# Compressed softmax moved forward, the last branch by tiles, and half of each norm's turning given to transposing transfers

## The chip, the cores and the metric

One NeuronCore of a Trainium2 chip runs the whole program. The metric is the device time of one execution in microseconds. The kernel before took 1357.85 us, the median of 3 runs (1355.42 to 1359.24).

## The reference

Two layers work on 256 tokens of width 1024, in fp32. Cut to what matters here, a layer is:

```python
h = h + 0.5 * swiglu(rms_norm(h, norm_g[i, 0]), ffn1_wi[i], ffn1_wo[i])
n = rms_norm(h, norm_g[i, 1])
... = split_cols(n @ w_in[i], IN_SPLITS)
ya = diff_attention(aq, ak, av, ...)
yb = nsa_attention(bq, bkc, bvc, bks, bvs, bkw, bvw, sigmoid(bgate), ...)
yc = swa_sink_attention(cq, ck, cv, ...)
merged = (sigmoid(ga) * (ya @ w_branch[i, 0]) + sigmoid(gb) * (yb @ w_branch[i, 1])
          + sigmoid(gc) * (yc @ w_branch[i, 2]))
h = h + merged @ w_out[i]
h = h + 0.5 * swiglu(rms_norm(h, norm_g[i, 2]), ffn2_wi[i], ffn2_wo[i])
h = h + sigmoid(rms_norm(h, norm_g[i, 3]) @ w_ple_gate[i]) * (p[i] @ w_ple[i])
```

A last `rms_norm` follows. In `nsa_attention` (branch B) a query attends to three sets of keys: 15 compressed blocks (`o_c`), selected blocks (`o_s`) and a window (`o_w`); their outputs are added, each under its gate. The compressed keys and values come from `gelu(blk @ w1) @ w2`, so they exist only after a product over the keys of all tokens.

## The kernel before, in words

**Tiles.** The 256 tokens are two tiles of 128 (`t` = 0 and 1). An operand of a product is held as a high and a low part (`split`: ScalarE rounds the high part, VectorE subtracts), and a product of two such operands is three matmuls (`mul3`, L234: high x high, high x low, low x high). Weights come in pieces of 128 x 1024 (`raw`, 4 buffers) by SP's queue, and each piece is split into `wh` (ScalarE, L228) and `wl` (VectorE, L223), 6 buffers each; `fetch` runs two pieces ahead.

**Products.** `product` (L305) goes through the contraction in steps. Tile 0 takes block `step`, tile 1 block `step - skew`, so that the beginning and the end of a product belong to one tile. When a tile's last block is done, its `done` function is called with a higher priority; then comes the next step. A norm's operand must have the model dimension on the partitions, so the residual sum `h` has to be turned: `residual` (L372) adds a product's 512 columns to `h`, calls `norm.turn(t, c)` (L343: four TensorE transposes into a bank `nt`, then `turned`, L330: four scalings on ScalarE, four subtractions on VectorE) and squares the columns for the norm's sum. The scale of the norm itself is applied later, to the product's result.

**The FFN** turns its gated values another way: `turn_by_dma` (L436) copies the high and the low 16 bits of each fp32 apart (`cut`, VectorE), SP issues a transposing DMA for each (`flip`), and `collect` puts the halves together again (`whole`, VectorE) when the next group of columns is done.

**The attention beside the products.** While projection and gate products run, attention units are emitted beside them: a `Flow` (L156) steps generators. Each call of `flow.tick()`, once for every three matmuls, moves each lane on by its pace (`PACE_B` for branch B); `flow.join(side)` steps until a side is finished. `attend_b` (L839) works through six units (group g, tile t, key sets), the softmax of one ahead of the weighting of the one before. At the end of a tile's last key set it waits for the compressed keys (`kc`, made by `compressed`, L736, in a second lane at pace 1.0), runs `attend_cmp(t)` (L803: scores `sc`, softmax `pc`, transpose `pct` to `pcT`) if the tile hasn't one, spreads `pcT` over the heads (`own`, L830), weights, and gathers `y_ps` into `yB[t]`. One PSUM bank holds `y_ps`.

**Order.** `attention` (L504) emits the projections, then branch 0 (differential), the compression, branch 2 (window with sinks) and last branch 1 (B). A branch is, for each half of the columns, a gate product `gate` (from the norm) and a product `br` (from `yT`); `mix` multiplies and adds to `merged`. In the last branch both gate products come first, then the join, then both `br` products, each over both tiles with a skew of 4; `mix` there also transposes `merged` (`mt`) and splits it into `mT`, the operand of the output product `wo`, whose `done` feeds the next norm. The program's order is only a priority: a planner in the framework, which estimates durations, lays down the order of instructions of each engine, and each engine then follows that order.

Of the kernel before, what the change touches and what calls it, by code (L numbers as in the profile page):

```python
# [10 lines left out]
F32 = mybir.dt.float32  # L11
F32R = mybir.dt.float32r
U16 = mybir.dt.uint16
# [17 lines left out]
AHEAD = 2  # L31
RAWS = 4
WBUFS = 6
PACE_A, PACE_B, PACE_C = 0.75, 0.75, 0.6

# [118 lines left out]
class Flow:  # L156
# [19 lines left out]
                    lane[1] -= 1.0  # L176
                    self.step(lane)

    def join(self, side):
        while any(s is side for lane in self.lanes.values() for s, _ in lane[0]):  # L180
            for lane in self.lanes.values():
                if lane[0]:
                    self.step(lane)
# [3 lines left out]
def trunk(ctx: ExitStack, tc: tile.TileContext, a: dict, out: bass.AP, index: list):  # L187
# [105 lines left out]
    def last_product(lhs, nk, done, name, w):  # L293
# [8 lines left out]
                done(t, ps, s)  # L302
        return run

    def product(lhs, nk, done, name, w, skew=SKEW):  # L305

        def run():
            ps = [None] * NT
            for step in range(nk + skew):
                for t, k in ((0, step), (1, step - skew)):  # L310
                    if 0 <= k < nk:
                        wh, wl = w(k)
                        if k == 0:
                            ps[t] = product_bank(f"{name}{t}")
                        xh, xl = lhs(t, k)
                        mul3(ps[t][:, :w.width], xh, xl, wh, wl, k == 0, k == nk - 1)
                        if k == nk - 1:
                            with tc.high_priority(offset=150):
                                done(t, ps[t])
                        flow.tick()  # L320
        return run


    class Norm:
# [16 lines left out]
                                               T[:, 0, k + m, :].bitcast(F32), op0=ALU.mult, op1=ALU.subtract)  # L341

        def turn(self, t, c):  # L343
            ps = tp_bank("nt")
            transposes(ps, [h[:, t, 512 * c + 128 * k:512 * c + 128 * k + 128] for k in range(4)])
            self.turned(t, 4 * c, ps)
# [82 lines left out]
            queue.dma_start(out[t * 128:(t + 1) * 128, 512 * k:512 * k + 512], y[k])  # L429


    def halves(x):

        return x.bitcast(U16).rearrange("p (n w) -> p n w", w=2)

    def turn_by_dma(pool, src, m):  # L436


        cut = stage("cut").bitcast(U16).rearrange("p (w n) -> p w n", w=2)
        flip = pool.tile([128, 2, 4, 128], U16, tag="flip", bufs=3, name="flip")  # L440
        for w in range(2):
            nc.vector.tensor_copy(cut[:, w, :128 * m], halves(src)[:, :128 * m, w])
            nc.sync.dma_start(flip[:, w, :m], cut[:, w, :128 * m], transpose=True)

        def collect():
            whole = stage("whole")
            for w in range(2):
                tc.keep_in_program_order(nc.vector.tensor_copy(  # L448
                    halves(whole)[:, :128 * m, w], flip[:, w, :m].rearrange("p a b -> p (a b)")))
            return whole[:, :128 * m].rearrange("p (k q) -> p k q", q=128)  # L450
        return collect

    def ffn(i, n, norm, after, aside=None):
        pool = None
        gT, held, pending = [None] * NT, {}, {}

        def begin():
            nonlocal pool
            pool = phase("ffn")
            for t in range(NT):  # L460
                gT[t] = pool.tile([128, 2, NF, 128], F32R, name=f"gT{t}")

        def collect(t):
            if t in pending:
                first, m, whole = pending.pop(t)
                split(gT[t][:, 0, first:first + m, :], gT[t][:, 1, first:first + m, :], whole())

        def gated(f):
            def done(t, ps):
                collect(t)  # L470
                if f % 2 == 0:
                    held[t] = pool.tile([128, 512], F32, tag="gated", bufs=4, name="gated")
                act = pool.tile([128, 256], F32, tag="act", bufs=3, name="act")
                nc.scalar.activation(act, ps[:, :256], AF.Silu, scale=norm.r(t))  # L474
                nc.vector.tensor_tensor(held[t][:, 256 * (f % 2):256 * (f % 2) + 256], act, ps[:, 256:], op=ALU.mult)  # L475
                if f % 2 or f == FG - 1:
                    first, m = f - f % 2, 2 * (f % 2 + 1)
                    pending[t] = 2 * first, m, turn_by_dma(pool, held[t], m)
            return done

        def gathered(t, k):
            if k == 8:
                collect(t)
            return gT[t][:, 0, k, :], gT[t][:, 1, k, :]

        steps = []

        def beside():
            if not steps:
                steps.append(aside(pool))  # L490
            next(steps[0])

        yield begin
        for f in range(FG):
            yield product(norm.lhs, NK, gated(f), "ff", streamed(i, f"{n}{f}", 512), 2 if aside and f == 0 else SKEW)
            if aside and f in (4, 5, 8):
                yield beside
        for c in range(2):
            if aside and c == 1:
                yield beside  # L500
            yield product(gathered, NF, after(c), "fo", streamed(i, f"{n}o{c}", 512))


    def attention(i, norm, after):  # L504
# [205 lines left out]
        def compress():  # L710
# [14 lines left out]
            for kv in range(2):  # L725
                for k in range(16):
# [3 lines left out]
                    nc.tensor.matmul(o, both, wh, start=k == 0, stop=False)  # L730
                    nc.tensor.matmul(o, both, wl, start=False, stop=k == 15)
                    flow.tick()
            c_sb[0] = pool.tile([128, 512], F32, name="c_sb")
            nc.vector.tensor_copy(c_sb[0][:64], c_ps[:64])

        def compressed():  # L736
# [44 lines left out]
            vc[0] = pool.tile([128, 1, 128], F32R, name="vc")  # L781
            values(vc[0], v_ps[:, :64], None)
            kc[0] = kt

        def weighted(y_ps, v, T, start, stop):

# [11 lines left out]
            v = tmp.rearrange("p (m q) -> p m q", m=2)  # L798
            split(y[:, 0, 2 * g:2 * g + 2, :], y[:, 1, 2 * g:2 * g + 2, :], v)

        yB, pcT = [None] * NT, {}

        def attend_cmp(t):  # L803
            s_ps = tp_bank("sc")
# [34 lines left out]
        def attend_b():  # L839
# [33 lines left out]
            def second(u, p):  # L873
                g, t, ss = u
                if yB[t] is None:
                    yB[t] = y_tile("yB")
                if ss[0] == 0:
                    y_ps[g, t] = y_bank("yb")
                for x in ss:
                    for k in range(t + 1):  # L880
                        T = turned([p[:, j, x, :] if t == 0 else p[:, j, 128 * k:128 * k + 128] for j in range(4)])
                        yield
                        weighted(y_ps[g, t], vB[0][:, x, k, g], T.rearrange("p x j q -> p x (j q)"), x == 0 and k == 0, False)
                        yield
                if ss[-1] == 1:
                    if t not in pcT:
                        while kc[0] is None:
                            yield
                        yield from attend_cmp(t)
                    T = own(t, g)  # L890
                    yield
                    weighted(y_ps[g, t], vc[0][:, 0], T.rearrange("p x j q -> p x (j q)"), False, True)
                    gather(yB[t], y_ps[g, t], g)
                    yield

            yield from pipelined([(g, t, ss) for t, sets in ((0, [(0, 1)]), (1, [(0,), (1,)])) for g in range(2) for ss in sets], first, second)
# [57 lines left out]
        def branch(b, yT, side, last=False):  # L954
# [32 lines left out]
            if last:  # L987
                for c in range(2):
                    yield gated(c, both[c][0])
                yield lambda: flow.join(sides[side])  # L990
                for c in range(2):
                    yield mixed(c, both[c][1])
            else:
                for c in range(2):
                    yield gated(c, both[c][0])
# [236 lines left out]
```

## Time and profile before

| | |
|---|---|
| median of 3 runs | 1357.85 us (1355.42 to 1359.24) |
| profiled execution | 1356.52 us, span 1354.7 us from the first to the last instruction |
| TensorE (PE) busy | 1331.4 us, 98% of the span, 6414 matmuls |
| weight loads of TensorE (PEld) | 1096.5 us, 81% |
| VectorE (DVE) busy | 947.4 us, 70% |
| ScalarE (ACT) busy | 782.2 us, 58% |
| mean granted clock of TensorE | 0.995 |

A matmul's record is longer than its turn, since matmuls are pipelined and their ends are modelled; what one costs in a stream is read from the starts of two neighbours. "Idle before" is the engine's idle time just ahead of an instruction, and the arrow names what ended it.

### The profile page before, as it was taken

The numbers are of one execution on the slowest core, as the hardware profiler recorded it, in microseconds if no ns is written. First come the engines' busy times: TensorE is split into PE (matmuls) and PEld (weight loads), VectorE is DVE, ScalarE is ACT, GpSimd is POOL, SyncE is SP. The second block draws the span as 40 slices with busy tenths as digits, with TensorE's granted clock in tenths as the row PEclk, the third lists the DMA queues.
The fourth block names the chain that finished last, engine by engine and source line by source line (L and its number), as shares of the span: only waits on it lengthen the run. The fifth ranks groups of instructions, "written<-read, shape, count | busy, mean of one in ns | idle before, by whom it ended". The sixth has DMA issues, their size and how long they took to land.

```text
span 1354.7 us, 18246 instructions
## 1 busy us (share of the span) xinstructions
PE 1331.4 (98%) x6414; PEld 1096.5 (81%) x6414; DVE 947.4 (70%) x1795; ACT 782.2 (58%) x1382; POOL 18.5 (1%) x36
## 2 busy tenths in 40 slices
PE   9999999999998999999999999999999989999997
PEld 7778888887886788888888888888788868888886
DVE  7677566768887767665767765577697776767565
ACT  7555455668655655544755544566795645545454
POOL 0000000000000000000000000000000000000000
PEclk9999999999999999999999999999999989999999
DMA  8797665444642577775567765645456425887662
GB/s 306 205 275 224 194 226 169 152 166 155 231 154 64 185 201 220 206 221 180 189 198 216 229 202 193 227 151 177 162 186 205 140 65 184 220 222 210 194 204 84
DMA packets 121993, 257.14 MB, mean 190 GB/s; under 512 B 56944, under 2 KB 62500, under 8 KB 121902
## 3 DMA queue, kind: packets, MB, share of 16 engines
q1 hardware_dynamic: 121150, 254.34, 60.5%
q0 software_dynamic: 320, 1.08, 0.3%
q8 instruction: 50, 0.82, 0.2%
q10 hardware_dynamic: 432, 0.56, 0.1%
q14 instruction: 41, 0.34, 0.1%
HBM read 243.33 MB, written 1.08 MB: 180 GB/s over the span
## 4 chain that ended last, share of the span: by engine, by line
PE 92%; DVE 3%; DMA 2%; ACT 2%; issue 1%; SPq 0%; POOLq 0%; POOL 0%; DVEq 0%; ACTq 0%
PE ff L236 11%; PE ff L237 11%; PE ff L235 11%; PE fo L236 6%; PE fo L235 6%; PE fo L237 6%; PE gate L235 3%; PE gate L237 3%; PE gate L236 3%; PE s L537 3%; PE A L236 2%; PE A L235 2%; PE A L237 2%; PE br L236 1%; PE br L235 1%; PE br L237 1%
## 5 line engine op out<-in xcount | busy, mean ns | idle before, releaser
L223 DVE TENSOR_TENSOR wl<-raw,wh 128x1024 fp32r<-128x1024 f32 (+1 forms) x448 | 539.8, 1213 | 176.5 <-ACT wh L228 169.3
L228 ACT ACTIVATE wh<-raw 128x1024 fp32r<-128x1024 f32 (+1 forms) x448 | 467.6, 1050 | 231.6 <-PE fo L237 84.9
L236 PE MATMUL ff<-wl,nT 128*128 128x512 f32 x704 | 273.6, 390 | 2.0 <-DVE wl L223 1.9
L237 PE MATMUL ff<-wh,nT 128*128 128x512 f32 x704 | 273.4, 390 | 0.0
L235 PE MATMUL ff<-wh,nT 128*128 128x512 f32 x704 | 270.8, 391 | 0.0
L236 PEld LDWEIGHTS ff<-wl,nT 128*128 128x128 f32 x704 | 132.2, 188 | 31.3 <-DVE wl L223 4.0
L235 PEld LDWEIGHTS ff<-wh,nT 128*128 128x128 f32 x704 | 132.4, 188 | 29.3 <-ACT wh L228 0.8
L237 PEld LDWEIGHTS ff<-wh,nT 128*128 128x128 f32 x704 | 132.3, 188 | 27.1
L236 PE MATMUL fo<-wl,gT 128*128 128x512 f32 x352 | 134.2, 392 | 0.0
L237 PE MATMUL fo<-wh,gT 128*128 128x512 f32 x352 | 133.7, 389 | 0.0
L235 PE MATMUL fo<-wh,gT 128*128 128x512 f32 x352 | 132.5, 389 | 0.0
L474 ACT ACTIVATE act<-ff,stats 128x256 f32<-128x256 f32 x88 | 41.4, 472 | 86.0 <-PE ff L237 85.8
L475 DVE TENSOR_TENSOR gated<-act,ff 128x256 f32<-128x256 f32 x88 | 36.6, 417 | 65.0 <-ACT act L474 65.0
L235 PEld LDWEIGHTS fo<-wh,gT 128*128 128x128 f32 x352 | 66.1, 188 | 13.9
L235 PE MATMUL gate<-wh,nT 128*128 128x512 f32 x192 | 77.0, 403 | 0.0
L237 PEld LDWEIGHTS fo<-wh,gT 128*128 128x128 f32 x352 | 66.1, 188 | 13.3
L236 PEld LDWEIGHTS fo<-wl,gT 128*128 128x128 f32 x352 | 66.1, 188 | 13.3
L236 PE MATMUL gate<-wl,nT 128*128 128x512 f32 x192 | 75.9, 395 | 0.0
L237 PE MATMUL gate<-wh,nT 128*128 128x512 f32 x192 | 75.8, 395 | 0.0
L228 ACT ACTIVATE gT<-whole 128x512 fp32r<-128x512 f32 (+1 forms) x48 | 28.4, 591 | 62.8 <-DVE whole L448 62.6
L548 ACT ACTIVATE p<-p,st 128x128 f32<-128x128 f32 (+1 forms) x128 | 56.7, 445 | 11.4 <-DVE st L546 11.0
L448 DVE COPY whole<-flip 128x512 uint16<-128x512 uint16 (+1 forms) x96 | 38.2, 434 | 12.8 <-DMA flip<-cut 12.2
(301 smaller groups left out, 2003.2 us busy)
## 6 DMA issues: line engine op xcount, KB each, us to landing
raw<-in_wst SPq DMA_DIRECT2D x438, 512.0 KB, 4.4
band<-table SPq DMA_DIRECT2D x10, 512.0 KB, 4.9
raw<-in_wbv SPq DMA_DIRECT2D x4, 420.0 KB, 3.2
flip<-cut SPq DMA_TRANSPOSE x96, 4.0
xt<-in_xt SPq DMA_DIRECT2D x4, 256.0 KB, 5.2
raw<-in_wst SPq DMA_DIRECT2D x4, 256.0 KB, 3.5
h<-in_x SPq DMA_DIRECT2D x2, 512.0 KB, 7.9
band<-table POOLq DMA_DIRECT2D x2, 512.0 KB, 6.7
```

The costliest lines, as they stand in the source:

```text
L223: nc.vector.tensor_tensor(o, x, y, op=ALU.subtract)
L228: nc.scalar.activation(hi, src, AF.Copy)
L235: nc.tensor.matmul(ps, xh, wh, start=start, stop=False)
L236: nc.tensor.matmul(ps, xh, wl, start=False, stop=False)
L237: nc.tensor.matmul(ps, xl, wh, start=False, stop=stop)
L448: tc.keep_in_program_order(nc.vector.tensor_copy(halves(whole)[:, :128 * m, w], flip[:, w, :m].rearrange("p a b -> p (a b)")))
L474: nc.scalar.activation(act, ps[:, :256], AF.Silu, scale=norm.r(t))
L475: nc.vector.tensor_tensor(held[t][:, 256 * (f % 2):256 * (f % 2) + 256], act, ps[:, 256:], op=ALU.mult)
L537: nc.tensor.matmul(o, q[r, x, qb[m], t * 128:(t + 1) * 128], kk, start=x + y == 0, stop=x == 1)
L548: nc.scalar.activation(p[j], p[j], AF.Exp, bias=st[:, j:j + 1], scale=-1.0, accum_out=st[:, n + j:n + j + 1])
```

## The change

The diff makes four edits.

- `attend_cmp(t)` of both tiles is stepped at the end of `compressed`, in the second lane; `attend_b` now waits until `pcT[t]` is there. `PACE_B` goes from 0.75 to 0.72, and `c_sb` shares the buffers of `th`.
- The last branch's `br` products go by tiles: `tile(0)` (both halves of the columns) once both groups of `yB[0]` are gathered (`readyB[0] == 2`), then the full join, then `tile(1)`. The weight pieces of both halves are read twice.
- `Norm.turn` with `c == 0` no longer uses TensorE: it calls `turn_by_dma` on `h`'s first 512 columns and puts the collect and `turned` off by 12 steps of `product` (`later`, `on_time`).
- `flip` moves to the pool that lives through the program, with 2 buffers in place of 3.

```diff
-PACE_A, PACE_B, PACE_C = 0.75, 0.75, 0.6
+PACE_A, PACE_B, PACE_C = 0.75, 0.72, 0.6
...
-    def join(self, side):
-        while any(s is side for lane in self.lanes.values() for s, _ in lane[0]):
+    def join(self, side, ready=lambda: False):
+        while not ready() and any(s is side for lane in self.lanes.values() for s, _ in lane[0]):
...
+    deferred = []
+
+    def later(steps, act):
+
+        deferred.append([steps, act])
+
+    def on_time():
+        for d in deferred:
+            d[0] -= 1
+        while deferred and deferred[0][0] <= 0:
+            deferred.pop(0)[1]()
+
...
             for step in range(nk + skew):
+                on_time()
...
+        flip = base.tile([128, 2, 4, 128], U16, tag="flip", bufs=2, name="flip")
...
         def turn(self, t, c):
+            if c == 0:
+                whole = turn_by_dma(h[:, t, :512], 4)
+                later(12, lambda: self.turned(t, 0, whole().rearrange("p k q -> p (k q)")))
+                return
...
-        flip = pool.tile([128, 2, 4, 128], U16, tag="flip", bufs=3, name="flip")
...
-            c_sb[0] = pool.tile([128, 512], F32, name="c_sb")
+            c_sb[0] = pool.tile([128, 512], F32, tag="th", bufs=4, name="c_sb")
...
             kc[0] = kt
+            yield
+            for t in range(NT):
+                yield from attend_cmp(t)
...
-                    if t not in pcT:
-                        while kc[0] is None:
-                            yield
-                        yield from attend_cmp(t)
+                    while t not in pcT:
+                        yield
...
                     gather(yB[t], y_ps[g, t], g)
+                    readyB[t] += 1
...
                 for c in range(2):
                     yield gated(c, both[c][0])
+                ws = [streamed(i, f"br{b}{c}", 512) for c in range(2)]
+
+                def tile(t):
+                    for c in range(2):
+                        ps = product_bank(f"br{t}")
+                        for k in range(4):
+                            wh, wl = ws[c](k)
+                            mul3(ps, yT[t][:, 0, k, :], yT[t][:, 1, k, :], wh, wl, k == 0, k == 3)
+                            flow.tick()
+                        with tc.high_priority(offset=150):
+                            both[c][1](t, ps)
+
+                yield lambda: flow.join(sides[side], lambda: readyB[0] == 2)
+                yield lambda: tile(0)
                 yield lambda: flow.join(sides[side])
-                for c in range(2):
-                    yield mixed(c, both[c][1])
+                yield lambda: tile(1)
```

## Rows read from the trace of the kernel before

**Rows 1.** The page, busy time by engine, and the chain that ended last.
```profile
PE 1331.4 (98%) x6414; PEld 1096.5 (81%) x6414; DVE 947.4 (70%) x1795; ACT 782.2 (58%) x1382; POOL 18.5 (1%) x36
...
PE 92%; DVE 3%; DMA 2%; ACT 2%; issue 1%; SPq 0%; POOLq 0%; POOL 0%; DVEq 0%; ACTq 0%
```

**Rows 2.** Timeline of PE at one turned block: start, duration, what, idle before.
```profile
461.13 0.39 PE L236 MATMUL wo<-wl,mT 128*128 128x512 f32 x1
461.35 0.39 PE L237 MATMUL wo<-wh,mT 128*128 128x512 f32 x1
461.59 0.60 PE L243 MATMUL nt<-ident,h 128*128 128x128 f32 x4
461.94 0.48 PE L235 MATMUL wo<-wh,mT 128*128 128x512 f32 x1
462.25 0.40 PE L236 MATMUL wo<-wl,mT 128*128 128x512 f32 x1
```

**Rows 3.** Stretches: length, busy PE, PEld, DVE, ACT, POOL; clock, DMA share, GB/s.
```profile
350.00:410.00 60.00, 60.00 (x307) 49.35 (x306) 45.64 (x109) 33.99 (x63) 0.00 (x0) 1.00 0.51 171
410.00:450.00 40.00, 33.89 (x166) 26.09 (x165) 32.87 (x66) 22.06 (x44) 0.00 (x0) 1.00 0.29 93
450.00:470.00 20.00, 20.00 (x97) 16.55 (x96) 14.32 (x26) 14.17 (x28) 0.55 (x1) 1.00 0.56 183
1080.00:1120.00 40.00, 34.45 (x156) 27.26 (x155) 31.20 (x64) 20.14 (x41) 0.00 (x0) 0.91 0.31 97
```

**Rows 4.** Timeline of PE, end of the attention of layer 0.
```profile
422.25 0.50 PE L788 MATMUL yb<-pT,vB 128*128 128x512 f32 x1
425.57 0.33 PE L243 MATMUL pct<-ident,pc 128*128 128x128 f32 x1 [2.81 <-DVE pc L822]
...
427.65 0.50 PE L787 MATMUL yb<-pcT,vc 128*128 128x512 f32 x1 [0.45 <-ACT pcT L228]
...
430.71 0.47 PE L787 MATMUL yb<-pT,vB 128*128 128x512 f32 x1 [0.47 <-DVE yt L797]
...
445.31 1.09 PE L243 MATMUL mt<-ident,merged 128*128 128x128 f32 x8 [0.63 <-DVE merged L969]
446.66 0.50 PE L235 MATMUL wo<-wh,mT 128*128 128x512 f32 x1 [0.25 <-ACT mT L231]
```

**Rows 5.** Timeline of PE, the same place in layer 1.
```profile
1090.25 0.50 PE L788 MATMUL yb<-pT,vB 128*128 128x512 f32 x1
1094.10 0.48 PE L243 MATMUL pct<-ident,pc 128*128 128x128 f32 x1 [3.35 <-DVE pc L822]
```

**Rows 6.** Groups by line: count, then busy us, mean ns, idle before.
```profile
L243 PE MATMUL nt<-ident,h 128*128 128x128 f32 x112 | 16.8, 272 | 0.0
```

**Rows 7.** The page's group of `whole`, and the view of tile `flip` (ns min/median/max).
```profile
L448 DVE COPY whole<-flip 128x512 uint16<-128x512 uint16 (+1 forms) x96 | 38.2, 434 | 12.8 <-DMA flip<-cut 12.2
...
L443 SPq DMA_TRANSPOSE flip<-cut x96: 1179/1210/2118, 31.4 to 1261.6; - x96
...
DMA to landing us min/median/max: 2.3/4.0/7.4
```

**Rows 8.** Timeline, from the output product to the next FFN in layer 0.
```profile
456.57 0.69 DVE L377 SCALAR_TENSOR_TENSOR h<-wo,h 128x512 f32<-128x512 f32 x1 [0.40 <-PE wo L237]
...
467.30 0.39 PE L235 MATMUL ff<-wh,nT 128*128 128x512 f32 x1
```

**Rows 9.** Timeline around 65 us.
```profile
64.73 0.39 PE L235 MATMUL ff<-wh,nT 128*128 128x512 f32 x1
65.17 0.45 DVE L448 COPY whole<-flip 128x512 uint16<-128x512 uint16 x1 [0.26 <-DMA flip<-cut]
...
66.79 0.50 PE L236 MATMUL ff<-wl,nT 128*128 128x512 f32 x1 [1.68 <-DVE wl L223]
```

**Rows 10.** Tile `pc` alone, by stretches: length, busy PE, PEld, DVE, ACT.
```profile
410.00:450.00 40.00, 0.33 (x1) 0.14 (x1) 1.69 (x6) 0.29 (x1) 1.00 0.29 93
```

**Rows 11.** Waits of PE: total us, times, longest.
```profile
PE ff L236 <- DVE wl L223: 1.9, 2, 1.7
```

More of the change, by code (lines that the diff above doesn't have):

```diff
@@ L321, in product, with halves, turn_by_dma, collect @@
         return run
+    def halves(x):
+        return x.bitcast(U16).rearrange("p (n w) -> p n w", w=2)
+    def turn_by_dma(src, m):
+        cut = stage("cut").bitcast(U16).rearrange("p (w n) -> p w n", w=2)
+        flip = base.tile([128, 2, 4, 128], U16, tag="flip", bufs=2, name="flip")
+        for w in range(2):
+            nc.vector.tensor_copy(cut[:, w, :128 * m], halves(src)[:, :128 * m, w])
+            nc.sync.dma_start(flip[:, w, :m], cut[:, w, :128 * m], transpose=True)
+        def collect():
+            whole = stage("whole")
+            for w in range(2):
+                tc.keep_in_program_order(nc.vector.tensor_copy(
+                    halves(whole)[:, :128 * m, w], flip[:, w, :m].rearrange("p a b -> p (a b)")))
+            return whole[:, :128 * m].rearrange("p (k q) -> p k q", q=128)
+        return collect
     class Norm:
@@ L429, in finished @@
             queue.dma_start(out[t * 128:(t + 1) * 128, 512 * k:512 * k + 512], y[k])
[L432 to L439, printed above, removed]
-        flip = pool.tile([128, 2, 4, 128], U16, tag="flip", bufs=3, name="flip")
[L441 to L451, printed above, removed]
     def ffn(i, n, norm, after, aside=None):
@@ L477, in done @@
                     first, m = f - f % 2, 2 * (f % 2 + 1)
-                    pending[t] = 2 * first, m, turn_by_dma(pool, held[t], m)
+                    pending[t] = 2 * first, m, turn_by_dma(held[t], m)
             return done
@@ L799, in gather @@
             split(y[:, 0, 2 * g:2 * g + 2, :], y[:, 1, 2 * g:2 * g + 2, :], v)
-        yB, pcT = [None] * NT, {}
+        yB, pcT, readyB = [None] * NT, {}, [0] * NT
         def attend_cmp(t):
```

## The prediction

> **What bounds the kernel now.** I read the page's busy line and its chain first [rows 1]: TensorE is busy 1331.4 of 1354.7 us, and the chain that ended last is 92% PE. In the long products one 512-column matmul starts some 0.23 us after the other, with no wait between [rows 2]. So the time falls only where TensorE gets less to do, or where it stands still. For the second I read the busy time by stretches [rows 3]: TensorE is full in 350:410 and 450:470, but idle for 6.1 us in 410:450 and 5.6 us in 1080:1120, the end of the attention in either layer. The rows inside these stretches [rows 4, 5] name the waits: the transpose of the compressed softmax (`pct`) waits 2.81 us for VectorE's `pc` L822, a `yb` matmul behind it waits 0.45 us for `pcT`, and at the end `mt` waits 0.63 us for `merged` and `wo` 0.25 us for `mT`.
>
> **Part 1, transposes off TensorE.** Seven norms (four of layer 0, three of layer 1; the last one of all is not turned) times two tiles of tokens lose the four `nt` transposes of the first 512 columns. Of the 112 on TensorE [rows 6] half go, 14 groups of four. What a group costs is read from starts [rows 2]: it starts at 461.59, the next product matmul at 461.94, the one behind that at 462.25: 0.66 us in place of one pitch of 0.23, so 0.43 to 0.44 us, and 14 x 0.44 = 6.2 us. TensorE is full there and nothing comes in their place, so this counts in full: -6.2 us.
>
> Added for each group: two `cut` and two `whole` copies on VectorE, and two transposing DMAs on SP. The FFN's gated values go the same way already, with 96 such DMAs [rows 7]: a `whole` copy takes 0.43 us (I take the same for a `cut`), an issue holds SP for 1.21 us, the landing comes 4.0 us after the issue (2.3 to 7.4). VectorE gets 56 copies, 56 x 0.43 = 24 us; it is busy for 947.4 of 1354.7 us [rows 1], and in 450:470, the tightest of the stretches concerned, for 14.3 of 20 us [rows 3], to which 1.7 us come for each of the two turned blocks. SP gets 28 issues of 1.21 us; weight loads queued behind them on SP are late by as much, which the raw buffers already loaded cover; without that cover a pair would cost up to 2.4 us. ScalarE and VectorE still do the four scalings and four subtractions of each half tile, now from SBUF; I cost that difference at nothing.
>
> Is the path in time? The collect is put off by 12 steps. The tightest place lies between the output product `wo` and the next FFN: the sum h starts at 456.57 and takes 0.69 us, the first FFN matmul starts at 467.30 [rows 8]. From 457.3: first cut 0.4, two issues 2.4 (the second cut lies beside the first), landing 2.8 after the second issue ends (4.0 less 1.2), two copies 0.9, scaling and subtraction some 2.3: 466.1, 1.2 us ahead of the need. With the latest landing, 7.4, it is 469.5, 2.2 us late. Behind a late landing the `whole` copies wait in VectorE's order, and the weight splits (`wl`) behind them. In the trace `whole` waits 12.2 us over 96 copies [rows 7], and one such wait reached TensorE: two starts 2.06 us apart at 64.73, where `wl` stood behind a waiting `whole` [rows 9]. The ends of this cost are nothing and 14 x 2.06 = 28.9 us. I take 1 us in all, near the low end, since it lies nearest to the rows of the same operation: 96 copies made one stall of 2 us, so 28 more make a third of one, and the rest is for the three tight boundaries (two from `wo` to an FFN, one from layer 0's gated addition to layer 1's FFN).
>
> The Trainium skill ("VectorE: DVE Perf Modes", section "Rules for kernel authors") speaks against this edit: a 128x128 transpose belongs on TensorE where a PSUM destination will do, and goes by the DMA crossbar otherwise; its section "The three transpose paths" gives 390 against 1309 ns. By its two figures each of the 56 turned blocks would lose 0.9 us, an estimate of 51 us if all of it lay open. The rows above bear that out for the duration of the path (0.66 us against some 9), not for what it costs while other products cover it.
>
> **Part 2, compressed softmax forward.** `attend_cmp(1)` stood in the attention's own lane, inside the second tile's units; now it follows `attend_cmp(0)` at once, in the lane of the compression. The instructions are the same; they move to where TensorE is full whatever VectorE does (45.6 of 60 us busy in 350:410 [rows 3]), which hides the 1.7 us that the `pc` operations take on VectorE [rows 10]; were VectorE full there, they would cost just that. What goes: the wait at `pct`, 425.57 - 422.25 - 0.23 = 3.1 us in layer 0 and 1094.10 - 1090.25 - 0.23 = 3.6 us in layer 1 [rows 4, 5], and the wait for `pcT`, 0.45 us a layer. In layer 1 the granted clock is 0.91 in this stretch, against 1.00 in layer 0 [rows 3]: after the longer standstill TensorE ran at the lower level, 1.2 GHz, for a while. That should go with the wait; I count nothing for it. What is late next is the last unit's softmax; with the `pc` operations gone from among its own it is earlier, and branch matmuls of tile 0 can fill.
>
> **Part 3, last branch by tiles.** Tile 0's 24 branch matmuls need only `yB` of tile 0 and now come before the join; tile 1's 24 follow. `wo` starts with tile 0, whose `mT` is then ready a whole tile earlier, so the waits of `mt` and `wo` go: 0.63 + 0.25 = 0.9 us a layer [rows 4], covered by tile 1's matmuls (24 x 0.23 = 5.5 us). Both weight pieces are held over two tiles: four of the six split buffers, which leaves two for `wo` ahead. Its third piece can be split once tile 1 has used the first, and the second half of tile 1 (2.7 us) covers that; uncovered it would cost about as much.
>
> Parts 2 and 3 together: 3.1 + 0.45 + 0.9 = 4.5 us in layer 0, 3.6 + 0.45 + 0.9 = 5.0 in layer 1, 9.5 in all. Bounds: nothing (another wait steps in), and all idle time of the two stretches, 11.7 us, with a fifth more that the modelled ends hide and the clock's part, about 15. I take 9.5.
>
> PACE_B 0.72 for 0.75, one `flip` buffer less (the two tiles never hold more than two) and `c_sb` in buffers of another name: the pace shifts the attention by 4% of its steps, inside covered work; I cost the three at nothing, with 2 us to either side in the range.
>
> **Sum.** The profiled execution took 1356.52 us (span 1354.7): 1356.5 - 6.2 - 9.5 + 1.0 = 1341.8. It lies 1.3 us under the median of the runs, 1357.85; on that scale 1343.1.
>
> **Rivals.**
> (a) The end of the attention refills: there is one bank for `yb`, so a unit's matmuls wait until the one before is gathered (0.47 us at 430.71 [rows 4]), and the last unit's softmax becomes the late one. For it: VectorE is busy 32.9 of 40 us there [rows 3]. Against: its work there gets less. Only the transposes are gained: 1357.85 - 6.2 + 1.0 = 1352.6.
> (b) The transfers are late at the tight boundaries, so that the longer path lies open there: 2.2 us at each of three, 6.6 us, eat part 1: 1357.85 - 9.5 - 6.2 + 6.6 = 1348.8. Against it: the 1.2 us of margin at the median landing. It is the way in which the rule quoted above from the Trainium skill would come true here.
> (c) The edit doesn't do what it says: the order on each engine comes from a planner, which may leave the compressed softmax late, and (b) eats the rest: about 1357. For it: `pct` ran behind all gate products though its lane is stepped among them.
> (d) Slower: each collect stands ahead of a weight split on VectorE and waits for its landing, so that TensorE stands still in all 14 places as at 64.73 [rows 9]. It decides from (6.2 + 9.5 + 4.1)/14 = 1.4 us a place; at 2.06 us the time is 1357.85 - 15.7 + 28.9 = 1371.1. Against it: the FFN's matmuls waited for `wl` only 1.9 us in all [rows 11], beside 96 such copies.
>
> **How the numbers follow.** Forecast 0.58, (a) 0.17, (b) 0.08, (c) 0.08, (d) 0.09. The forecast's own range is 1337 to 1348: down by 5 (all idle time) and 1 (free collects), up by half of the attention's gain. For 8 in 10, with 2 us more for the pace below, up to (c) above and without (d): 1334 to 1356. A change under 0.3% (4.1 us) can't be told from none here. Faster: the forecast, (b) and most of (a), 0.79; within 0.3%: (c) and the rest of (a), 0.12; slower: (d), 0.09.
>
> **What would show it.** The changed profile should have 56 `nt` transposes, 124 transposing DMAs, `pct` ahead of the last gate matmuls with no wait at it, a granted clock of 1.00 at the end of layer 1's attention, `mt` of tile 0 ahead of tile 1's branch matmuls, and some 6 us less of TensorE's busy time. I am wrong if product matmuls wait several us for a `wl` behind `whole`, or if the two stretches keep over 3 us of idle time each.

## The result, and the profile after

The changed kernel takes 1348.4 us (median of 4 runs, 1345.44 to 1349.38); the kernel before took 1357.55 us beside it (4 runs). The ratio is 0.993, interval 0.9908 to 0.9951. That is faster by 9.15 us, where 14.8 were forecast; the time lies 0.4 us above the forecast's own range of 1337 to 1348 us and inside the wider one, 1334 to 1356. The profiled execution took 1345.44 us, the least of the four, with a span of 1343.7 us: 11.1 us under the profiled execution of before.

The page of the changed kernel, its busy line, its chain, the line of the `whole` copies and that of the transposing transfers; the first two answer to [rows 1], the third and fourth to [rows 7]:

```profile
PE 1321.1 (98%) x6358; PEld 1087.4 (81%) x6358; DVE 965.0 (72%) x1851; ACT 784.5 (58%) x1382; POOL 19.6 (1%) x36
...
PE 88%; DVE 6%; DMA 3%; issue 1%; ACT 1%; SPq 0%; POOLq 0%; POOL 0%; DVEq 0%; ACTq 0%
...
L352 DVE COPY whole<-flip 128x512 uint16<-128x512 uint16 (+1 forms) x124 | 49.6, 438 | 19.0 <-DMA flip<-cut 18.6
...
flip<-cut SPq DMA_TRANSPOSE x124, 4.1
```

56 matmuls are gone from TensorE, 56 operations have come to VectorE, and 124 transfers turn blocks, as predicted. TensorE's busy time fell by 10.3 us, more than the 6 of the transposes: without part 1 (`softmax_tiles` below, 1325.7 us) it is already 5.7 us lower, with as many matmuls as before. VectorE's part of the chain has doubled, 3% to 6%.

Busy time of each engine in stretches of the changed kernel (start:end and length in us, busy time of each engine with its instructions, granted clock, DMA share, GB/s). It answers to [rows 3]; the stretch of layer 1 is taken 5 us wider at the front here, since the work lies earlier:

```profile
350.00:410.00 60.00, 60.00 (x309) 49.71 (x308) 47.99 (x116) 34.99 (x62) 0.00 (x0) 1.00 0.54 176
410.00:450.00 40.00, 35.85 (x180) 28.16 (x180) 31.00 (x63) 21.86 (x47) 0.00 (x0) 1.00 0.32 99
450.00:470.00 20.00, 19.17 (x87) 15.24 (x86) 17.36 (x39) 14.44 (x30) 1.11 (x2) 1.00 0.76 224
1075.00:1120.00 45.00, 40.84 (x202) 32.27 (x201) 33.72 (x65) 24.79 (x46) 0.00 (x0) 1.00 0.36 110
```

The two ends of the attention stand idle for 4.15 and 4.16 us. 450:470, full before, has lost 0.83 us, and VectorE is busy there for 17.36 us in place of 14.3. What TensorE waits for in the changed kernel, longest sums first, cut to what matters here (sum in us, times, longest):

```profile
PE mt L243 <- DVE merged L988: 3.4, 2, 1.7
PE yb L807 <- DVE yt L817: 1.9, 4, 0.8
...
PE ff L236 <- DVE wl L223: 1.5, 2, 1.3
PE nt L243 <- DVE h L415: 1.4, 2, 0.7
PE wo L235 <- ACT mT L231: 1.4, 2, 0.7
PE ff L235 <- ACT nT L370: 1.2, 3, 0.6
PE wo L236 <- DVE wl L223: 1.2, 2, 0.6
```

The wait of `pct` has gone, but `mt` now waits up to 1.7 us [rows 4: 0.63], and three waits are new: `nt` for the sum h, FFN matmuls for `nT`, and `wo` for a weight part `wl`, 0.6 us in each layer. The last is there without part 1 too (1.2 us in two places).

**An account by starts.** Summed over all matmuls, I took the distance from each start to the next, less the pitch of its kind in a stream, that is the distance between two starts where nothing waits (0.227 us for 512 columns, 0.11 to 0.13 for the narrow ones). What is over is time lost to waits, to changes from one kind of matmul to another or to a lower clock. In us:

| | before | softmax and tiles, no turning | changed | changed, no copies |
|---|---|---|---|---|
| sum of the pitches | 1308.4 | 1308.4 | 1302.3 | 1302.3 |
| lost in 350:450 (end of attention, layer 0) | 10.2 | 5.7 | 6.6 | 5.7 |
| lost in 450:500 (`wo` to FFN, layer 0) | 0.2 | 0.1 | 1.5 | 0.0 |
| lost in 650:700 (gated addition to FFN) | 0.2 | 0.1 | 1.1 | 0.0 |
| lost in 1050:1150 (the same two places, layer 1) | 11.1 | 5.4 | 7.7 | 5.3 |

The columns in the middle and at the right are experiments told of below. By their pitches (56 x 0.109) the transposes saved 6.1 us, the forecast's 6.2. The attention saved 4.5 and 5.7 us where it was changed alone; the 11.1 of before hold a stretch of 6.8 us, from 1092.7, in which the granted clock was at its lower level, 1.2 GHz. Then the turning took back 0.9 + 1.4 + 1.0 + 2.3 = 5.6 us in these four stretches.

### The profile page after: what moved, and what is told of

The parts are those of the page before. It is cut to its first block, busy times and chain, and to the rows that moved or that the text cites. A ratio compares the mean times of both kernels' runs of the same rounds, so it can differ in the third digit from the quotient of the medians.

```text
span 1343.7 us, 18223 instructions
## 1 busy us (share of the span) xinstructions
PE 1321.1 (98%) x6358; PEld 1087.4 (81%) x6358; DVE 965.0 (72%) x1851; ACT 784.5 (58%) x1382; POOL 19.6 (1%) x36
## 4 chain that ended last, share of the span: by engine, by line
PE 88%; DVE 6%; DMA 3%; issue 1%; ACT 1%; SPq 0%; POOLq 0%; POOL 0%; DVEq 0%; ACTq 0%
PE ff L237 10%; PE ff L235 10%; PE ff L236 10%; PE fo L237 6%; PE fo L236 6%; PE fo L235 6%; PE gate L235 3%; PE gate L237 3%; PE gate L236 3%; PE s L554 2%; DVE wl L223 2%; PE A L235 2%; PE A L236 2%; PE A L237 2%; PE br L236 1%
## 5 line engine op out<-in xcount | busy, mean ns | idle before, releaser
L228 ACT ACTIVATE wh<-raw 128x1024 fp32r<-128x1024 f32 (+1 forms) x448 | 468.3, 1050 | 229.5 <-PE fo L237 81.9
L237 PE MATMUL ff<-wh,nT 128*128 128x512 f32 x704 | 273.5, 390 | 0.0
L237 PEld LDWEIGHTS ff<-wh,nT 128*128 128x128 f32 x704 | 132.3, 188 | 27.2
L237 PE MATMUL fo<-wh,gT 128*128 128x512 f32 x352 | 134.8, 389 | 0.0
L237 PEld LDWEIGHTS fo<-wh,gT 128*128 128x128 f32 x352 | 66.1, 188 | 13.5
L237 PE MATMUL gate<-wh,nT 128*128 128x512 f32 x192 | 76.1, 396 | 0.0
L352 DVE COPY whole<-flip 128x512 uint16<-128x512 uint16 (+1 forms) x124 | 49.6, 438 | 19.0 <-DMA flip<-cut 18.6
```

Of the source, the lines that this page charges most:

```text
L228: nc.scalar.activation(hi, src, AF.Copy)
L237: nc.tensor.matmul(ps, xl, wh, start=False, stop=stop)
L352: tc.keep_in_program_order(nc.vector.tensor_copy(halves(whole)[:, :128 * m, w], flip[:, w, :m].rearrange("p a b -> p (a b)")))
```

## The experiments

Each ratio is to the kernel before, run beside it on the same chip; its medians there lay between 1357.2 and 1358.2 us.

**1. The change taken apart.** Part 1 alone on the kernel before (in this run and the next three `c_sb` and `flip` have the buffers of the changed kernel, for room):

```diff
+            if c == 0:
+                whole = turn_by_dma(h[:, t, :512], 4)
+                later(12, lambda: self.turned(t, 0, whole().rearrange("p k q -> p (k q)")))
+                return
```

> The kernel before with part 1 alone (the first 512 columns of each norm turned by transposing transfers; c_sb in the buffers of th, for room). By the prediction's terms: -6.2 for the transposes, +1.0 for the collects, 1352.3 us on the scale of 1357.5. By the trace of the changed kernel (the new standstills at the three boundaries, 1.5 + 1.1 + 1.5 us between starts, belong to this part): -6.1 + 4.1, about 1355.5. TensorE's idle time ahead of nt and ff at 460, 670 and 1120 us is there in the second case and not in the first.

Measured: 1355.16 us against 1358.06, ratio 0.9982 (0.9972 to 0.9992). A gain of 2 to 3 us, not the 5.2 of the forecast's terms. At the end of layer 0's attention `mt` waits 2.75 us in it, where it waited 0.63 before [rows 4]; no copy of part 1 stands near, and part 2 alone shows the same wait (below), so this isn't the copies' price.

Part 2 alone, the compressed softmax in the other lane, with `PACE_B` 0.72:

```diff
             kc[0] = kt
+            yield
+            for t in range(NT):
+                yield from attend_cmp(t)
...
-                    if t not in pcT:
-                        while kc[0] is None:
-                            yield
-                        yield from attend_cmp(t)
+                    while t not in pcT:
+                        yield
```

> The kernel before with part 2 alone (compressed softmax in the lane of the compression, PACE_B 0.72; both br products over both tiles as before, turning by TensorE). By the prediction's terms: 3.1 + 3.6 + 0.9 = 7.6 us less, 1349.9. Rival: the part that moves the end of the attention is the order by tiles, and a softmax that comes earlier only lets VectorE's other work be the late one: 1356 or more. Either way no wait of pct at the end of the attention.

Measured: 1347.89 us, 0.992 (0.9908 to 0.9932), 10 us faster.

Part 3 alone, the last branch by tiles (its last lines; `tile` is as in the change):

```diff
...
+                yield lambda: flow.join(sides[side], lambda: readyB[0] == 2)
+                yield lambda: tile(0)
                 yield lambda: flow.join(sides[side])
-                for c in range(2):
-                    yield mixed(c, both[c][1])
+                yield lambda: tile(1)
```

> The kernel before with part 3 alone (last branch by tiles). By the prediction's terms: 0.9 us a layer, 1355.7. Rival, from the changed kernel's trace (mt waits 2.1 us and wo 0.96 us behind tile 1's last branch matmuls, more than before): going by tiles uses up tile 0's wo matmuls as filler ahead of tile 1, so that nothing is left to cover tile 1's chain from br over merged and mt to mT: no gain or slower, 1357.5 to 1360.

Measured: 1351.82 us, 0.995 (0.9936 to 0.9963), 6 us faster; I had given it 1.8.

Parts 2 and 3 without part 1:

```diff
-            if c == 0:
-                whole = turn_by_dma(h[:, t, :512], 4)
-                later(12, lambda: self.turned(t, 0, whole().rearrange("p k q -> p (k q)")))
-                return
```

> The changed kernel without part 1 (turning by TensorE as before). By the prediction's terms 1357.5 - 9.5 = 1348.0. By the trace of the changed kernel, where the ends of the attention lost 3.1 and 3.9 us of standstill: 1350.5. If part 1 is worth what the sum of terms says, this is 5.2 us slower than the changed kernel's 1348.4, 1353.6; if part 1 gives back 4.1 of its 6.1 us, it is 2 us slower.

Measured: 1346.46 us, 0.991 (0.9896 to 0.9923), 12 us faster. Two things follow. Part 1 adds nothing measurable to this. And the gains of parts 2 and 3 don't add up: 10 and 6 us alone, 12 together. TensorE's idle time at the two ends of the attention, in the profiled executions (us):

| | before | part 2 alone | part 3 alone | both |
|---|---|---|---|---|
| 410:455 (layer 0) | 6.1 | 5.4 | 5.7 | 3.2 |
| 1075:1120 (layer 1) | 5.6 | 2.3 | 3.8 | 3.2 |

In layer 1 each edit alone takes away much of the standstill, and the gains overlap. In layer 0 neither takes away much alone: each left what the other would have removed. The longest waits at the end of layer 0's attention, first with part 2 alone, then with part 3 alone (rows of the timeline of TensorE: start, duration, what, idle before):

```profile
444.06 1.95 PE L243 MATMUL mt<-ident,merged 128*128 128x128 f32 x12 [2.75 <-DVE merged L984]
```

```profile
427.75 0.47 PE L243 MATMUL pct<-ident,pc 128*128 128x128 f32 x1 [3.34 <-DVE pc L835]
```

With part 2 alone `pct` no longer waits, but TensorE has nothing beside the last `mt` and waits 2.75 us there: the forecast's "what is late next". VectorE does both `th` additions and a weight split there before the first `merged`; in layer 1 of the same run `merged` comes right behind the first `th`, and `mt` waits 0.60 us. With part 3 alone the wait of `pct` stays in layer 0; in layer 1 it is 0.98 us. Why the planner's order differs between the layers wasn't looked into.

**2. Where the gain of part 1 goes.** The changed kernel once more, unaltered, as the yardstick beside the next three:

> The changed kernel itself, beside the three others of this chip: 1348, and slower than softmax_tiles (the changed kernel without part 1: 0.991 of before), so that part 1 is worth nothing or less on top of parts 2 and 3, though the sum of the prediction has it at -5.2 us.

Measured: 1346.44 us against 1358.15, 0.9919 (0.9905 to 0.9932).

Turning by transfers only in the norms that follow an FFN, where another product covers it; the norms behind `wo` and behind the gated addition turn on TensorE as before:

```diff
-            if c == 0:
+            if c == 0 and self.row % 4 in (1, 3):
```

> The changed kernel with the transposing transfers only in the norms that follow an FFN (4 norms, 8 groups); the norms behind wo and behind the gated addition (3 norms, 6 groups) turn by TensorE as before. If what part 1 gives back is lost at those three boundaries: softmax_tiles' time less 8 x 0.44 = 3.5 us, some 1343, faster than the changed kernel by 4 to 5. If each collect costs something wherever it stands: no faster than softmax_tiles, 1346 or more.

Measured: 1342.86 us, 0.9892 (0.9877 to 0.9907). Half of the edit is worth more than all of it: of 14 turned groups 6 were given up (2.6 us of transposes), and the time still fell by 3.6 us (the slowest of these 4 runs took 1344.12 us, the fastest of the changed kernel beside them 1345.38).

No copies and no transfers (the first 512 columns go on unturned, so part of the computation is left out):

```diff
-                whole = turn_by_dma(h[:, t, :512], 4)
-                later(12, lambda: self.turned(t, 0, whole().rearrange("p k q -> p (k q)")))
+                later(12, lambda: self.turned(t, 0, h[:, t, :512]))
```

> The changed kernel with the 12-step deferral kept, but the scalings read h itself: no cut and whole copies and no transposing transfers in the norms (the first 512 columns are not turned, which is left out here). If VectorE's copies or the landing hold TensorE up at the boundaries: softmax_tiles' time less all of 6.2 us, some 1340.5. If it is the order that comes of collecting 12 steps late: about the changed kernel's time, 1346 to 1348, and the standstills at 460, 670 and 1120 us stay.

Measured: 1340.19 us, 0.9871 (0.9857 to 0.9885).

All copies, no transfers (the cut copies write `flip` themselves; these columns stay unturned):

```diff
-    def turn_by_dma(src, m):
+    def turn_by_dma(src, m, dma=True):
...
-            nc.vector.tensor_copy(cut[:, w, :128 * m], halves(src)[:, :128 * m, w])
-            nc.sync.dma_start(flip[:, w, :m], cut[:, w, :128 * m], transpose=True)
+            o = cut[:, w, :128 * m] if dma else flip[:, w, :m].rearrange("p a b -> p (a b)")
+            nc.vector.tensor_copy(o, halves(src)[:, :128 * m, w])
+            if dma:
+                nc.sync.dma_start(flip[:, w, :m], cut[:, w, :128 * m], transpose=True)
...
-                whole = turn_by_dma(h[:, t, :512], 4)
+                whole = turn_by_dma(h[:, t, :512], 4, False)
```

> The changed kernel with all four copies of each group and the deferral, but the cut copies write the flip tile and no transfer is issued (again the columns stay unturned). If late landings are what costs (the prediction's rival b): 1340.5 to 1342. If VectorE's copies or the order cost it: the changed kernel's time.

Measured: 1347.64 us, 0.9929 (0.9916 to 0.9942). So the price of the turning is 6 us, and it is paid for VectorE's four copies a group (for their time, or for the order that the planner lays with them), not for the transfers, their issues or their landing. The stretches around the boundaries say the same. Busy time in 455:475 (`wo` to FFN), 660:690 (gated addition to FFN) and 1115:1140 (`wo` to FFN of layer 1), columns as above; first without transfers, then without copies:

```profile
455.00:475.00 20.00, 19.18 (x88) 15.15 (x87) 16.83 (x40) 13.98 (x30) 1.12 (x2) 1.00 0.64 211
660.00:690.00 30.00, 29.44 (x133) 23.82 (x132) 23.87 (x50) 20.11 (x40) 1.10 (x2) 1.00 0.42 141
1115.00:1140.00 25.00, 24.17 (x110) 19.33 (x109) 18.29 (x41) 16.35 (x32) 1.11 (x2) 1.00 0.53 169
```

```profile
455.00:475.00 20.00, 20.00 (x93) 16.55 (x92) 13.68 (x30) 12.97 (x26) 2.03 (x2) 1.00 0.70 229
660.00:690.00 30.00, 30.00 (x138) 24.80 (x136) 21.15 (x39) 18.19 (x34) 1.48 (x2) 1.00 0.59 183
1115.00:1140.00 25.00, 25.00 (x116) 20.69 (x115) 17.10 (x36) 16.58 (x31) 2.03 (x2) 1.00 0.60 194
```

TensorE (first busy number) stands still only where the copies are. With turning behind FFNs alone it is full in all three as well. VectorE (third number) isn't full in any of them.

**3. Can the copies go elsewhere?** The norms' copies on GpSimd:

```diff
-    def turn_by_dma(src, m):
+    def turn_by_dma(src, m, cutter=nc.vector, joiner=nc.vector):
...
-                whole = turn_by_dma(h[:, t, :512], 4)
+                whole = turn_by_dma(h[:, t, :512], 4, nc.gpsimd, nc.gpsimd)
```

> The changed kernel with the cut and whole copies of the norms (56 of 304 microsecond-scale copies) on GpSimd in place of VectorE. If VectorE's time at the boundaries is what part 1 costs: near the kernel without copies, 1340 to 1342, mt wait back to 0.7 us. Rival: GpSimd takes longer for a strided 16-bit copy than VectorE's 0.43 us, by so much that the turned half comes too late for the first FFN matmuls: 1347 or more, with ff waiting for nT.

Measured: 1359.78 us against 1358.24, 1.0007 (0.9997 to 1.0018): all that the change had gained is lost. (The kernel has 248 of these copies, 56 of them the norms', not 304.) GpSimd at the first boundary of this kernel, and TensorE's waits there:

```profile
457.47 3.03 POOL L346 COPY cut<-h 128x512 uint16<-128x512 uint16 x2 [15.18 <-DVE h L415]
460.45 1.46 POOL L352 COPY whole<-flip 128x512 uint16<-128x512 uint16 x2
```

```profile
463.58 0.66 PE L243 MATMUL nt<-ident,h 128*128 128x128 f32 x4 [1.73 <-DVE h L415]
...
466.67 0.79 PE L237 MATMUL ff<-wh,nT 128*128 128x512 f32 x1 [1.17 <-DVE nT L374]
```

The pair of cuts takes 3.03 us here in place of 0.75 on VectorE, and the wait of `nt` grows from 0.70 to 1.73 us. Behind these waits the granted clock falls as well (start:end and columns as above; the third number from the right is the clock):

```profile
465.30:472.10 6.80, 5.63 (x14) 4.09 (x14) 4.30 (x19) 3.82 (x10) 1.73 (x3) 0.50 0.35 133
```

That is TensorE's lower level, 1.2 GHz, and the clock reads 0.50 behind the other two boundaries too, in 680.3:687.1 and 1137.7:1144.5. By the account of starts some 7 us are lost at each boundary, standstill and clock together, where the changed kernel loses 1.1 to 1.5. At the end of layer 0's attention, where only one pair of cuts stood in the way, the move does help: `mt` waits 0.91 us in place of 1.71.

The cuts of the norm behind `wo` put off by four steps, to let `merged` pass them:

```diff
...
+                if self.row % 4 == 2:
+                    later(4, cut)
...
```

> The changed kernel with the cut copies behind wo put off by 4 steps (out of the high priority of done; the collect follows 8 steps later, so stands where it stood). If two cut copies ahead of tile 1's merged on VectorE make the longer mt wait (1.7 us against 0.7 without part 1): mt wait 0.7 again, 2 us less than the changed kernel, 1344.5. If the whole copies at the next FFN are what costs: the changed kernel's 1346.4.

Measured: 1344.84 us, 0.9906 (0.989 to 0.9921). The time came near what I expected, but not for my reason. The planner put the two cuts right behind h all the same, ahead of the additions that lead to `merged` (VectorE's timeline), and `mt` waits up to 1.7 us as in the changed kernel:

```profile
439.69 0.69 DVE L422 SCALAR_TENSOR_TENSOR h<-wo,h 128x512 f32<-128x512 f32 x1 [1.45 <-PE wo L237]
440.42 0.76 DVE L346 COPY cut<-h 128x512 uint16<-128x512 uint16 x2
```

What improved, by the account of starts, is the boundary from `wo` to the FFN: some 0.7 us lost in place of 1.5, in either layer.

**4. The pace, and the best mix.** The kernel that turns by transfers behind FFNs alone, with `PACE_B` back at 0.75:

```diff
-PACE_A, PACE_B, PACE_C = 0.75, 0.72, 0.6
+PACE_A, PACE_B, PACE_C = 0.75, 0.75, 0.6
```

> turn_after_ffn (1342.9, 0.9892 of before) with PACE_B 0.75 in place of 0.72. The prediction put the pace at nothing, with 2 us to either side: 0.988 to 0.991 of before. Rival: the pace decides where the units of branch B fall among the gate products, and with 0.75 the last unit is emitted before tile 0's branch matmuls, which shortens the end: under 0.988.

Measured: 1343.77 us, 0.9893 (0.988 to 0.9907), the same as with 0.72.

And both halves of the columns turned by transfers in the norm behind the second FFN, with the first half in the one behind the first:

```diff
-            if c == 0:
-                whole = turn_by_dma(h[:, t, :512], 4)
-                later(12, lambda: self.turned(t, 0, whole().rearrange("p k q -> p (k q)")))
+            if (c == 0 and self.row % 4 == 1) or self.row % 4 == 3:
+                whole = turn_by_dma(h[:, t, 512 * c:512 * c + 512], 4)
+                later(12, lambda: self.turned(t, 4 * c, whole().rearrange("p k q -> p (k q)")))
```

> turn_after_ffn (1342.9, 0.9892 of before), and in the norm between the second FFN and the gated addition the other 512 columns go by transposing transfers too (4 more groups off TensorE): the products pp lie between, and VectorE is not full there. If a group is worth its 0.44 us wherever VectorE has room: 1.8 us less, 1341.1, 0.988 of before. If the copies cost there too: 1343 or more, with matmuls of pp or pg waiting for wl.

Measured: 1341.74 us against 1357.22, 0.9886 (0.987 to 0.9903). It beats both kernels, the changed one by some 5 us; from the one that turns by transfers behind FFNs alone the intervals don't separate it.

## Why the prediction was right in direction and too large

**Part 1: right in what it takes off, wrong in what it costs.** 56 transposes saved 6.1 us of TensorE's stream. The step that failed is "I take 1 us in all" for the collects: it was 6 us (1340.2 without copies, 1346.4 with them), so the part is worth nothing on top of the others, and these 5 us are nearly all of the 5.3 by which the forecast's 1343.1 missed. I had priced landings. But they were early: in the changed kernel SP issues the two pairs at 440.95 and 459.20, and the pairs are read at 459.34 and 467.99 without an idle gap before the copy. VectorE's queue at the first boundary (start, duration, what, idle before):

```profile
457.54 1.22 DVE L223 TENSOR_TENSOR wl<-raw,wh 128x1024 fp32r<-128x1024 f32 x1
458.67 0.75 DVE L346 COPY cut<-h 128x512 uint16<-128x512 uint16 x2
459.34 0.79 DVE L352 COPY whole<-flip 128x512 uint16<-128x512 uint16 x2
460.02 1.21 DVE L223 TENSOR_TENSOR wl<-raw,wh 128x1024 fp32r<-128x1024 f32 x1
461.15 0.14 DVE L392 TENSOR_SCALAR stats<-stats 128x1 f32<-128x1 f32 x1
461.21 0.68 DVE L415 SCALAR_TENSOR_TENSOR h<-wo,h 128x512 f32<-128x512 f32 x1
461.81 1.21 DVE L223 TENSOR_TENSOR wl<-raw,wh 128x1024 fp32r<-128x1024 f32 x1
462.94 0.68 DVE L415 SCALAR_TENSOR_TENSOR h<-wo,h 128x512 f32<-128x512 f32 x1
```

and TensorE at its end:

```profile
462.39 0.60 PE L243 MATMUL nt<-ident,h 128*128 128x128 f32 x4
463.68 0.65 PE L243 MATMUL nt<-ident,h 128*128 128x128 f32 x4 [0.70 <-DVE h L415]
```

No row of VectorE has an idle time before it: for 6 us it works without a gap, and the last h stands behind 1.54 us of copies and three weight splits. The last transposes of the half that is still turned on TensorE wait 0.70 us for that h, and behind two FFN matmuls (at 461.82 and 462.15) the FFN's others stand behind those transposes. My sum had the right number for the stretch (14.3 + 2 x 1.7 = 17.7 us of 20; measured 17.36) and drew the wrong conclusion from it: a share under 100% is no room while the operations that come at the boundary stand in one queue. Nor was 450:470 the tightest of the stretches, as I had called it: in 455:475 of the kernel before VectorE was busy for 15.8 of 20 us.

The Trainium skill's rule ("VectorE: DVE Perf Modes", section "Rules for kernel authors") would leave 128x128 transposes on TensorE. At these three boundaries the runs agree with it (turning back six groups there gained 3.6 us); behind the FFNs, where another product is under way, they don't (eight groups left on transfers: 1342.9 us against 1346.5 with none, measured on two chips; 3.5 us were expected). The figures of the Trainium skill's section "The three transpose paths" on that page, which the prediction took for its 51 us, are latencies of one bf16 block; here the longer path isn't what costs. Rival (b), late landings, came to 1348.8 us and so next to the measured time, but that is chance: the run without transfers takes as long as the changed kernel.

**Parts 2 and 3: the size about right, by another division, and so in part by luck.** Forecast 4.5 us in layer 0 and 5.0 in layer 1; the account shows 4.5 and 5.7 without part 1. By the medians it is 12 us (10.5 to 14.1 from the interval), some 2 more than in the profiled executions. The likely reason is that the clock falls in more of the runs of before: the mean granted clock of its runs lay between 0.992 and 0.997, that of the four runs with parts 2 and 3 at 0.998. I had said that this part would go and counted nothing for it. What I had wrong is the division (7.6 for part 2's waits, 1.8 for part 3): alone they gain 10 and 6 us. I summed waits as if each would vanish on its own, and alike in both layers. They lie in one standstill at the end of the attention: in layer 1 either edit fills part of it, in layer 0 it takes both. Of the 0.45 us a layer for `pcT`, the wait stands in layer 0 alone; in layer 1 the `yb` behind `pct` starts at 1096.79 with no wait. Rival (a), a refilled end, holds in a weaker form: both stretches keep over 4 us idle, more than the 3 us that I had named as the mark of being wrong, and 3.2 each without part 1.

**The tail got worse, with part 1 most of all.** I had 0.9 us a layer go at `mt` and `wo`. In layer 0 `pct` runs at 387.22 and 404.83, before the gates end (before: at 395.68, among the gates too, and at 425.57, behind them), and `mt` of tile 0 runs ahead of tile 1's last branch matmuls, as predicted. But tile 1's own end stays. TensorE there, in the changed kernel:

```profile
441.16 0.39 PE L237 MATMUL br<-wh,yB 128*128 128x512 f32 x1
443.26 0.63 PE L243 MATMUL mt<-ident,merged 128*128 128x128 f32 x4 [1.71 <-DVE merged L988]
444.58 0.50 PE L235 MATMUL wo<-wh,mT 128*128 128x512 f32 x1 [0.69 <-ACT mT L231]
```

and the same place without part 1:

```profile
443.43 0.63 PE L243 MATMUL mt<-ident,merged 128*128 128x128 f32 x4 [0.69 <-DVE merged L984]
444.84 0.50 PE L235 MATMUL wo<-wh,mT 128*128 128x512 f32 x1 [0.78 <-ACT mT L231]
```

So even without part 1 neither wait goes: 0.69 and 0.78 us, after 0.63 and 0.25 before. The new wait of `wo` for `wl`, 0.6 us a layer, is the one that I had held to be covered: at 436.04 in the changed kernel `wo`'s third weight piece comes late, since its split on ScalarE waits for a branch matmul of tile 1 (3.07 us idle before it, ended by `br` L237).

VectorE ahead of `mt`, first in the changed kernel, then without part 1:

```profile
439.77 0.69 DVE L415 SCALAR_TENSOR_TENSOR h<-wo,h 128x512 f32<-128x512 f32 x1 [1.43 <-PE wo L237]
440.50 0.76 DVE L346 COPY cut<-h 128x512 uint16<-128x512 uint16 x2
441.18 0.68 DVE L987 SCALAR_TENSOR_TENSOR th<-th,br 128x512 f32<-128x512 f32 x1
...
441.84 0.68 DVE L987 SCALAR_TENSOR_TENSOR th<-th,br 128x512 f32<-128x512 f32 x1
442.43 0.68 DVE L988 TENSOR_TENSOR merged<-merged,th 128x512 f32<-128x512 f32 x1
```

```profile
440.96 0.69 DVE L411 SCALAR_TENSOR_TENSOR h<-wo,h 128x512 f32<-128x512 f32 x1 [1.45 <-PE wo L237]
441.86 0.69 DVE L983 SCALAR_TENSOR_TENSOR th<-th,br 128x512 f32<-128x512 f32 x1 [0.22 <-PE br L237]
442.59 0.69 DVE L984 TENSOR_TENSOR merged<-merged,th 128x512 f32<-128x512 f32 x1
```

Part 3 uses tile 0's `wo` matmuls as filler, so tile 0's h is ready before tile 1's branch is added up. With part 1 that h brings two cuts (0.76 us), which nobody needs for 18 us, ahead of the additions that TensorE waits for, and the planner then puts both `th` ahead of `merged`. Without part 1 `mt` waits 0.69 us, 1.02 us less. The rows divide this in halves: from the start of h to that of the first `th` it is 1.41 us in place of 0.90, and from there to `merged` 1.25 in place of 0.73. The forecast treated the parts as independent and had no term for this. Whether the cuts cause the swapped order stays open: with parts 2 and 3 in place it comes only in the runs whose cuts stand there on VectorE, but parts 1 and 2 alone have it in layer 0 too, with no cut near it.

**What held.** The clock in the profiled execution is 1.00 at the end of layer 1's attention (0.91 before), though not in every execution (last section); the pace is worth nothing; FFN products wait 1.5 us for `wl` in two places, 1.9 in two before [rows 11], the longest again near 66 us, so rival (d) is out.

What stays open: which operation makes the FFN late behind the gated addition (660:690), where its matmuls wait 0.2 to 0.3 us twice for ScalarE's `nT` with a `whole` pair close by. The loss (1.1 us) goes with the copies; the chain between wasn't taken apart.

## What to carry to other kernels

Price work that is moved to another engine by the queue of that engine at the place where the next stage waits for it, not by its busy share over a stretch: here four copies a group cost as much as the transposes that they replaced, and the exchange was worth it only where another product covered it. Waits that lie in one standstill aren't added up: find what ends it. Of two cures the second may bring little (here in layer 1), or neither much without the other (here in layer 0). When one edit makes a value early, look what that value triggers on a shared engine.

## What the runs showed of the hardware

**GpSimd.** A `cut` copy of 128x512 values of 16 bits takes a median of 616 ns there, up to 1691; on VectorE it takes 421. The groups of copies in that kernel:

```profile
L346 POOL COPY cut<-h x28: 608/616/1691, 156.1 to 1293.8; 128x512 uint16<-128x512 uint16 x28
...
L346 DVE COPY cut<-gated x96: 286/421/429, 31.7 to 1264.3; 128x512 uint16<-128x512 uint16 x80, 128x256 uint16<-128x256 uint16 x16
```

The three numbers are the shortest, the median and the longest in ns. VectorE beside them was slower too: a `wl` at 461.23 took 1.70 us in place of 1.22. Whether the two engines hinder each other wasn't measured by itself.

**The same standstill with and without a clock fall.** In two executions of the changed kernel TensorE is busy for as long around the end of layer 0's attention, and the granted clock differs; first the profiled execution, then the one of the repeat:

```profile
425.00:450.00 25.00, 21.01 (x97) 16.44 (x97) 16.15 (x27) 10.88 (x20) 0.00 (x0) 1.00 0.32 95
```

```profile
425.00:450.00 25.00, 21.00 (x92) 16.26 (x91) 15.94 (x27) 10.60 (x19) 0.00 (x0) 0.93 0.32 95
```

In the second the granted clock was at the lower level, 1.2 GHz, for 3.41 us from 445.0 and again from 1110.6, each time right behind the standstill at `mt`, and once more from 8.1, at the start of the program; its span is 1347.7 us against 1343.7. By the account of starts the two falls behind `mt` cost 1.5 us each. So the same wait costs more in one execution than in another, and much of the 4 us between runs of one kernel is of this kind.
